# Sixty-four-row products of a hybrid backbone, cut into 64x64 quarters of the TensorE array

## Chip, core and metric

The kernel runs on one core of a Trainium2 chip. The metric is the device time of one execution in microseconds, the median of three runs. Another time in this text is that of one profiled execution, and its span, which is the time from the first to the last recorded instruction.

## What is computed

A two-layer backbone works on 1024 latent and 256 context tokens (1280 in all) of width 1024, in fp32. Each layer normalizes and modulates the tokens, projects them, and gives the columns to four mixers (S5, mLSTM, differential attention, gated linear attention). One output projection and a squared-ReLU MLP follow. The parts that matter here, cut from the reference:

```python
# S5: 16 groups, 64 complex states and 16 channels each, two directions
bu_re = einsum('blgh,gph->blgp', u, bb_re)          # and bu_im
h = associative_scan(...)                            # h_t = lam * h_(t-1) + bu_t
y = einsum('blgp,ghp->blgh', h_re, c_re) - einsum('blgp,ghp->blgh', h_im, c_im)

# mLSTM: 4 heads of width 64, chunks of 128 tokens, two directions
c_chunk = einsum('bhcs,bhcsv,bhcsk->bhcvk', e, vc, kc)
# c_prev: the state before each chunk
sc  = einsum('bhctd,bhcsd->bhcts', qc, kc) * exp(dmat - m_t[..., None])
num = einsum('bhcts,bhcsv->bhctv', sc, vc) + a_int[..., None] * einsum('bhcvk,bhctk->bhctv', c_prev, qc)
den = sum(sc, -1) + a_int * einsum('bhck,bhctk->bhct', n_prev, qc)
h   = num / maximum(abs(den), exp(-m_t))[..., None]

def hybrid_layer(x_lat, x_ctx, ...):
    s5, ml, da, gl = s5_mixer(...), mlstm_mixer(...), diff_attention_mixer(...), gla_mixer(...)
    x = x + g1 * (concat([s5, ml, da, gl]) @ w_out)
    x = x + g2 * sq_relu_mlp(norm(x), mlp_w1, mlp_w2)
```

## The kernel before

The kernel is written as generators, one for each mixer, that record instructions in small steps; `beside` and `both` interleave the steps. A scheduler then places each engine's instructions by readiness and priority, so that the order on an engine isn't the order of the text: two products that stand side by side in a loop may end up apart.

The stages of a layer follow each other. The modulation and the norm come first, then the projections `z_steps` (tiles zp). In layer 0 the constants of S5 (`s5_prep`) are made beside them. S5 (`s5_mix`) and GLA (`gla_mix`) run beside the projections, too. Then attention (`da_mix`), mLSTM (`ml_mix`) and half of the output projection (wop, `p_out`) run side by side. The other half of the output projection follows, and the MLP (m1p and m2p, each weight as a sum of two parts, hence the three lines L1124 to L1126). During the MLP of layer 0 `split_side` steps the constants of S5 for layer 1 forward, one group in every eight weight tiles.

TensorE multiplies a stationary tile (up to 128 rows by 128 columns) with moving columns; rows are the partitions of both operands, the columns of the stationary tile become the partitions of the output. Most products use all 128 rows. Four kinds use 64, since two S5 groups, or two mLSTM heads, lie above each other in the 128 partitions:

- L267 in `s5_prep`, the S5 constants: `win` (64 rows, 128 columns) by 16 moving columns, into two banks s5pd, one for each half of the rows;
- L313 in `s5_mix.outputs`, the S5 outputs: `mout` (64 rows, 128 columns) by the states X, 160 moving columns in layer 0 and 128 in layer 1, added to the product of L308 in the two banks s5py;
- L804 in `ml_mix.scores`: keys by queries, 128 moving columns, banks mlst;
- L826 in `ml_mix.values`, the inter-chunk part: decayed queries (mlab) by the state C (mlC, 65 moving columns), added to the product of L821 in the two banks mlpn.

In each, the loop over the halves of the rows (`g2`, `R` or `hh`) is the innermost. The innermost lines of L313, for example:

```python
for g2 in range(2):
    R = slice(64 * g2, 64 * g2 + 64)
    pe.matmul(py[g2][:, 0:n], mout[R, d, r], X[R, d, r, c0:], start=False, stop=d == 1 and r == 1)
```

Others of the kernel's products use part of the array already: L788 (mlpu) and L518 (dapo) have 128 rows and 64 columns and alternate between the column halves, L1064 (glpo) has 64x64 quarters. Who reads the results of the four: ScalarE's copies L276 and L277 for s5pd, VectorE's L316 for s5py, L809 for mlst, L829 and L835 for mlpn.

Of the kernel before, what the change touches and what calls it, by code (L numbers as in the profile page):

```python
# [138 lines left out]
def s5_prep(env, P, l, s5s, s5v, nj=2):  # L139
# [4 lines left out]
    v, g, act, pe = nc.vector, nc.gpsimd, nc.scalar, nc.tensor  # L144
    dr = env.dram
    dt_ = lambda nm, sh: dr.tile(sh, F32, name=f"s5_{nm}{l}", tag=f"s5_{nm}{l}")
    o = Env()
# [63 lines left out]
    for j0 in range(0, 8, nj):  # L211
# [11 lines left out]
        while m < 160:  # L223
            n = min(m, 160 - m, 64)
# [10 lines left out]
        win = P.tile([128, 2, 2, nj, 8, 16], F32, tag="win", name="s5win", bufs=nj)  # L235
# [14 lines left out]
        for jj in range(nj):  # L250
            pt = env.bank("s5p", "s5pt")
# [8 lines left out]
        H2 = [slice(64 * g2, 64 * g2 + 64) for g2 in range(2)]  # L260
        pd = [env.bank("s5p", "s5pd") for _ in range(2)]
        for jj in range(nj):
            for d in range(2):
                c0 = 32 * d + 16 * jj
                for r, rhs in ((0, vv[:, 2, d, jj]), (1, cn[:, d, jj])):
                    for R, p in zip(H2, pd):
                        pe.matmul(p[:, c0:c0 + 16], win[R, d, r, jj].rearrange("p s h -> p (s h)"), rhs[R], start=r == 0, stop=r == 1)  # L267
        for jj in range(nj):
            c0 = 64 + 16 * jj
            for d in range(2):  # L270
# [7 lines left out]
        C = slice(32 * j0, 32 * j0 + 32 * nj)  # L278
# [6 lines left out]
def s5_mix(env, l, o, us5, dskip, gluw, glub, out_cb, need_ctx=True):  # L285
# [3 lines left out]
    v, g, act, pe = nc.vector, nc.gpsimd, nc.scalar, nc.tensor  # L289
    dr = env.dram  # L290
    c0 = 0 if need_ctx else 32
    n = 160 - c0
    gs5 = dr.tile([128, 16, 160], F32, name=f"gs5_{l}", tag=f"gs5_{l}")
    with tc.tile_pool(name=f"s5m{l}", bufs=1, side="right", reuse_waits="tile") as P:
# [8 lines left out]
        def outputs(j, mout, toep, X):  # L303

            Y = P.tile([128, 2, n], F32, tag="Y", name="s5Y", bufs=1)
            py = [env.bank("s5y", "s5py") for _ in range(2)]
            for g2 in range(2):
                pe.matmul(py[g2][:, 0:n], toep[:, g2], U[:, 2 * j + g2, c0:], start=True, stop=False)  # L308
            for d in range(2):
                for r in range(2):  # L310
                    for g2 in range(2):
                        R = slice(64 * g2, 64 * g2 + 64)
                        pe.matmul(py[g2][:, 0:n], mout[R, d, r], X[R, d, r, c0:], start=False, stop=d == 1 and r == 1)  # L313
            for g2 in range(2):
                gi = 2 * j + g2
                v.scalar_tensor_tensor(Y[:, g2, :], U[:, gi, c0:], dsk[:, gi:gi + 1], py[g2][:, 0:n], op0=ALU.mult, op1=ALU.add)  # L316
            y2 = P.tile([128, 2, n], F32, tag="y2", name="s5y2", bufs=1)
            act.activation(y2, Y, AF.Square)
            g.tensor_scalar(y2, y2, 0.044715, 1.0, op0=ALU.mult, op1=ALU.add)
            v.tensor_tensor(y2, y2, Y, op=ALU.mult)  # L320
            v.tensor_scalar(y2, y2, -25.0, None, op0=ALU.max)
            act.activation(y2, y2, AF.Exp, scale=-2.0 * math.sqrt(2.0 / math.pi))
            act.activation(y2, y2, AF.Ln, bias=1.0)
            act.activation(y2, y2, AF.Exp, scale=-1.0)
            v.tensor_tensor(y2, y2, Y, op=ALU.mult)
            nc.sync.dma_start(gs5[:, 2 * j:2 * j + 2, c0:], y2)
            yield 2

        todo = []
        for j in range(8):  # L330
# [6 lines left out]
            mout = P.tile([128, 2, 2, 128], F32, tag="mo", name="s5mo", bufs=2)  # L337
# [3 lines left out]
            X = P.tile([128, 2, 2, 160], F32, tag="X", name="s5X", bufs=2)  # L341
# [350 lines left out]
def ml_mix(env, l, gates, qk, V, O, convw, convb, gain, cmask, out_cb, need_ctx):  # L692
# [4 lines left out]
    v, g, act, pe = nc.vector, nc.gpsimd, nc.scalar, nc.tensor  # L697
# [3 lines left out]
    with tc.tile_pool(name=f"ml{l}", bufs=1, side="right", reuse_waits="tile") as P:  # L701
# [5 lines left out]
        qT = P.tile([128, 2, T], F32, name="mlqT")  # L707
        kT = P.tile([128, 2, T], F32, name="mlkT")
        big = lambda nm: P.tile([128, T + 3], F32, tag="big", name=nm, bufs=6)
        for i in (2, 0, 3, 1):  # L710
# [8 lines left out]
            n = T + 1 - t0  # L719
# [21 lines left out]
        with tc.tile_pool(name=f"mlw{l}", bufs=1, side="right", reuse_waits="tile") as P2:  # L741
# [56 lines left out]
            def scores(hp, c2):  # L798
                R_ = [slice(64 * hh, 64 * hh + 64) for hh in range(2)]
                pt = [env.bank("mls", "mlst") for _ in range(2)]  # L800
                for c in range(2):
                    t0 = 128 * (c2 + c)
                    for hh in range(2):
                        pe.matmul(pt[hh][:, 128 * c:128 * c + 128], kT[R_[hh], hp, t0:t0 + 128], qT[R_[hh], hp, t0:t0 + 128], start=True, stop=True)  # L804
                yield 1
                for hh in range(2):
                    for d in range(2):
                        e = S[hp]["E"][d, hh][:, c2:c2 + 2].rearrange("p a b -> p (a b)")
                        v.tensor_tensor(e, pt[hh][:, 0:256], e, op=ALU.mult)  # L809
                yield 1  # L810

            def values(hp, c2, tmp):
# [2 lines left out]
                pns = [env.bank("mlv", "mlpn") for _ in range(2)]  # L815
                cd = [(c, d) for c in range(c2, c2 + 2) for d in range(2)]
                o = lambda hh, c, d: pns[hh][:, 130 * (c - c2) + 65 * d:130 * (c - c2) + 65 * d + 65]

                for c, d in cd:
                    for hh in range(2):  # L820
                        pe.matmul(o(hh, c, d), s["E"][d, hh][:, c], vx[:, c, 2 * hp + hh], start=(c, d) == cd[0], stop=False)  # L821
                yield 1
                for c, d in cd:
                    for hh in range(2):
                        R_ = slice(64 * hh, 64 * hh + 64)
                        pe.matmul(o(hh, c, d), s["qa"][d][R_, 128 * c:128 * c + 128], s["C"][d][R_, c], start=False, stop=(c, d) == cd[-1])  # L826
                pns = [pn[:, 0:260].rearrange("p (c d e) -> p c d e", c=2, d=2) for pn in pns]
                for hh in range(2):
                    v.tensor_copy(dn[:, hh], pns[hh][:, :, :, 64])  # L829
# [883 lines left out]
```

## Time and profile before

| what | us |
|---|---|
| median of three runs (3724.34 to 3726.04) | 3724.48 |
| the profiled execution | 3719.97 |
| its span | 3718.2 |
| TensorE matmul (PE) busy | 3435.5 (92%) |
| TensorE weight load (PEld) busy | 2725.4 (73%) |
| VectorE (DVE) busy | 2228.8 (60%) |
| ScalarE (ACT) busy | 1309.4 (35%) |
| GpSimd (POOL) busy | 450.7 (12%) |

PE rows are matmuls and PEld rows the weight loads that belong to them; the two overlap, and matmuls overlap one another, so a busy PE isn't at its peak. A form like "64*128 64x16" reads: a stationary tile of 64 rows and 128 columns, and 64 rows of 16 moving columns. In a timeline neighbours of one kind are merged into a row with a count, and the time given is that from the start of the first to the end of the last.

### The profile page before, as it was taken

Reading aid. Unit: us, or ns where it says so; the run is one execution under the profiler, and the core shown is the slowest. Engines: PE = TensorE matmul, PEld = TensorE weight load, DVE = VectorE, ACT = ScalarE, POOL = GpSimd, SP = SyncE. Lnnn points to the kernel's source line nnn. Section 1 sums busy time; section 2 is a strip of 40 time slices with the busy share of each in tenths; the row PEclk is TensorE's granted clock in tenths of the full one; section 3 lists DMA queues with packets and bytes.
Section 4 is the critical chain, followed back from the end, with each engine's and each line's share of the span. In section 5 each row is a group of like instructions: output and inputs, shape, how many; then the busy total and the mean of one; then the engine's idle time right before and its main releaser. Section 6 shows DMA issues by size and latency. Waiting matters only on the chain. (4 is left out here: it accounts for less than half of the span.)

```text
span 3718.2 us, 53487 instructions
## 1 busy us (share of the span) xinstructions
PE 3435.5 (92%) x20338; PEld 2725.4 (73%) x20338; DVE 2228.8 (60%) x5455; ACT 1309.4 (35%) x2457; POOL 450.7 (12%) x520
## 2 busy tenths in 40 slices
PE   6989998798889999999999798988889899999998
PEld 3867767576658888888888476867677578888885
DVE  9654685877659855455544637486788543333334
ACT  4223434766542121212121522435676431222222
POOL 2121221222100000000000123120222000000000
PEclk8979999898899999999999998999889899999999
DMA  5665324655461221222111265314653611111112
GB/s 216 230 205 154 129 77 133 214 183 166 141 208 57 90 82 69 81 74 86 61 39 42 102 201 161 120 57 143 213 167 104 205 46 51 46 51 46 52 47 78
DMA packets 233959, 430.23 MB, mean 116 GB/s; under 512 B 47415, under 2 KB 135911, under 8 KB 233447
## 3 DMA queue, kind: packets, MB, share of 16 engines
q1 hardware_dynamic: 192806, 381.03, 31.2%
q10 hardware_dynamic: 35520, 30.52, 2.6%
q0 software_dynamic: 5376, 15.28, 1.2%
q8 instruction: 160, 2.62, 0.3%
q14 instruction: 97, 0.79, 0.1%
HBM read 316.88 MB, written 109.86 MB: 115 GB/s over the span
## 5 line engine op out<-in xcount | busy, mean ns | idle before, releaser
L1562 DVE SCALAR_TENSOR_TENSOR X<-m2p,mods,X 128x256 f32<-128x256 f32 (+1 forms) x512 | 345.7, 683 | 345.1 <-PE m2p L1126 344.6
L1115 ACT CAST whi<-raw 128x1024 fp32r<-128x1024 f32 x182 | 191.1, 1050 | 919.8 <-PE m2p L1125 638.0
L1124 PE MATMUL m2p<-hidhi,whi 128*128 128x512 f32 (+1 forms) x1280 | 473.8, 372 | 3.5 <-DVE X L1562 2.8
L1124 PE MATMUL m1p<-h2hi,whi 128*128 128x512 f32 (+1 forms) x1280 | 474.3, 371 | 0.2 <-ACT h2hi L1209 0.2
L1125 PE MATMUL m1p<-h2lo,whi 128*128 128x512 f32 (+1 forms) x1280 | 473.6, 370 | 0.0
L1125 PE MATMUL m2p<-hidlo,whi 128*128 128x512 f32 (+1 forms) x1280 | 473.1, 370 | 0.0
L1126 PE MATMUL m2p<-hidhi,wlo 128*128 128x512 f32 (+1 forms) x1280 | 472.2, 370 | 0.8 <-DVE wlo L1116 0.8
L1126 PE MATMUL m1p<-h2hi,wlo 128*128 128x512 f32 (+1 forms) x1280 | 472.6, 370 | 0.0
L1116 DVE TENSOR_TENSOR wlo<-raw,whi 128x1024 fp32r<-128x1024 f32 x182 | 224.7, 1235 | 313.2 <-ACT whi L1115 301.2
L1124 PEld LDWEIGHTS m2p<-hidhi,whi 128*128 128x128 f32 x1280 | 241.6, 189 | 59.6 <-issue 8.6
L1124 PEld LDWEIGHTS m1p<-h2hi,whi 128*128 128x128 f32 x1280 | 243.1, 190 | 46.2 <-ACT whi L1115 4.2
L1126 PEld LDWEIGHTS m2p<-hidhi,wlo 128*128 128x128 f32 x1280 | 241.2, 188 | 46.4 <-issue 3.4
L1125 PEld LDWEIGHTS m1p<-h2lo,whi 128*128 128x128 f32 x1280 | 243.4, 190 | 40.8 <-DVE h2lo L1210 0.8
L1126 PEld LDWEIGHTS m1p<-h2hi,wlo 128*128 128x128 f32 x1280 | 243.2, 190 | 40.3 <-issue 0.4
L1125 PEld LDWEIGHTS m2p<-hidlo,whi 128*128 128x128 f32 x1280 | 241.6, 189 | 42.0 <-issue 2.2
L1124 PE MATMUL zp<-hhi,whi 128*128 128x512 f32 (+1 forms) x664 | 254.2, 383 | 11.6 <-ACT zst L1237 9.6
L487 DVE TENSOR_SCALAR_CACHE_REDUCE das<-daps 128x512 f32<-128x512 f32 (+1 forms) x400 | 226.0, 589 | 58.4 <-PE daps L486 55.0
L1125 PE MATMUL zp<-hlo,whi 128*128 128x512 f32 (+1 forms) x664 | 251.2, 378 | 5.6 <-DVE hlo L1205 5.2
L1126 PE MATMUL zp<-hhi,wlo 128*128 128x512 f32 (+1 forms) x664 | 249.5, 376 | 0.0
L1576 DVE TENSOR_TENSOR rl<-rl,m1p 128x256 f32<-128x256 f32 (+1 forms) x160 | 100.8, 631 | 177.1 <-ACT rl L1575 177.1
L498 ACT ACTIVATE das<-das,danm 128x1280 f32<-128x1280 f32 x128 | 174.3, 1362 | 42.7 <-DVE danm L496 42.3
L486 PE MATMUL daps<-daqk,daqk 128*128 128x512 f32 (+1 forms) x400 | 153.3, 447 | 38.0 <-DVE das L487 36.6
(460 smaller groups left out, 6671.3 us busy)
## 6 DMA issues: line engine op xcount, KB each, us to landing
raw<-w SPq DMA_DIRECT2D x136, 512.0 KB
adaw<-ada_w SPq DMA_DIRECT2D x96, 512.0 KB
whl<-wsp SPq DMA_DIRECT2D x80, 512.0 KB
wsp<-whl SPq DMA_DIRECT2D x32, 512.0 KB
raw<-wz SPq DMA_DIRECT2D x30, 512.0 KB
daqk<-da_st SPq DMA_DIRECT2D x24, 640.0 KB
mlE<-ml_rows SPq DMA_DIRECT2D x16, 640.0 KB
xn<-xo SPq DMA_DIRECT2D x72, 128.0 KB
```

The source lines that it names most:

```text
L486: pe.matmul(p[:, 0:b - a], Q[m][:, 128 * qt:128 * qt + 128], K[m][:, a:b], start=True, stop=True)
L487: v.tensor_scalar(s[:, a:b], p[:, 0:b - a], -1.0, None, op0=ALU.mult, op1=ALU.min, accum_out=pm[:, i:i + 1])
L498: act.activation(s[:, :k1], s[:, :k1], AF.Exp, bias=nm[:, 0:1], scale=-1.0, accum_out=sm[m])
L1115: nc.scalar.copy(hi, raw)
L1116: nc.vector.tensor_tensor(lo, raw, hi.bitcast(F32), op=ALU.subtract)
L1124: pe.matmul(out, ah, bh, start=i == 0, stop=False)
L1125: pe.matmul(out, ah, bl, start=False, stop=False)
L1126: pe.matmul(out, al, bh, start=False, stop=i == n - 1)
L1562: nc.vector.scalar_tensor_tensor(X[b][:, m], p[:, :n], mod(l, 5, s)[:, m:m + 1], X[b][:, m], op0=ALU.mult, op1=ALU.add)
L1576: nc.vector.tensor_tensor(rl[:, :n], rl[:, :n], p[:, :n], op=ALU.mult)
```

## The change

Each of the four products is cut into two that have 64 of the 128 stationary columns each and write 64 partitions of the same bank. The loop over the column halves (`M`) stands outside the loop over the row halves, so that in the text four quarters follow each other: rows 0 to 63 and 64 to 127 with the first 64 columns, then both with the last 64. Operands, banks, sums and moving columns stay the same. The number of matmuls of these lines doubles: in both layers together 128, 128, 72 and 144 become 256, 256, 144 and 288.

```diff
@@ s5_prep
-                    for R, p in zip(H2, pd):
-                        pe.matmul(p[:, c0:c0 + 16], win[R, d, r, jj].rearrange("p s h -> p (s h)"), rhs[R], start=r == 0, stop=r == 1)
+                    for M in H2:
+                        for R, p in zip(H2, pd):
+                            pe.matmul(p[M, c0:c0 + 16], win[R, d, r, jj].rearrange("p s h -> p (s h)")[:, M], rhs[R], start=r == 0, stop=r == 1)
@@ s5_mix, outputs
+            H2 = [slice(64 * i, 64 * i + 64) for i in range(2)]
...
-                    for g2 in range(2):
-                        R = slice(64 * g2, 64 * g2 + 64)
-                        pe.matmul(py[g2][:, 0:n], mout[R, d, r], X[R, d, r, c0:], start=False, stop=d == 1 and r == 1)
+                    for M in H2:
+                        for g2 in range(2):
+                            pe.matmul(py[g2][M, 0:n], mout[H2[g2], d, r, M], X[H2[g2], d, r, c0:], start=False, stop=d == 1 and r == 1)
@@ ml_mix, scores
-                    for hh in range(2):
-                        pe.matmul(pt[hh][:, 128 * c:128 * c + 128], kT[R_[hh], hp, t0:t0 + 128], qT[R_[hh], hp, t0:t0 + 128], start=True, stop=True)
+                    for M in R_:
+                        for hh in range(2):
+                            pe.matmul(pt[hh][M, 128 * c:128 * c + 128], kT[R_[hh], hp, t0 + M.start:t0 + M.stop], qT[R_[hh], hp, t0:t0 + 128], start=True, stop=True)
@@ ml_mix, values
+                H2 = [slice(64 * i, 64 * i + 64) for i in range(2)]
...
-                    for hh in range(2):
-                        R_ = slice(64 * hh, 64 * hh + 64)
-                        pe.matmul(o(hh, c, d), s["qa"][d][R_, 128 * c:128 * c + 128], s["C"][d][R_, c], start=False, stop=(c, d) == cd[-1])
+                    for M in H2:
+                        for hh in range(2):
+                            pe.matmul(o(hh, c, d)[M], s["qa"][d][H2[hh], 128 * c + M.start:128 * c + M.stop], s["C"][d][H2[hh], c], start=False, stop=(c, d) == cd[-1])
```

Since the scheduler places the instructions, two places show what stands in TensorE's row now. The first is in the MLP of layer 0, at one group of the S5 constants (adap is the modulation of layer 1, s5pt a transpose; the lines below the change have moved by up to four). Before:

```order
L253 MATMUL s5pt<-ident,s5win 128x128 x4
L267 MATMUL s5pd<-s5vv,s5win 128x16
L267 MATMUL s5pd<-s5cn,s5win 128x16
L267 MATMUL s5pd<-s5vv,s5win 128x16
L267 MATMUL s5pd<-s5cn,s5win 128x16
L274 MATMUL s5pd<-s5vv,s5win 16x16
L274 MATMUL s5pd<-s5cn,s5win 16x16
L274 MATMUL s5pd<-s5vv,s5win 16x16
L274 MATMUL s5pd<-s5cn,s5win 16x16
L1124 MATMUL m1p<-h2hi_10593,whi 128x256
```

And now, at the same place:

```order
L253 MATMUL s5pt<-ident,s5win 128x128 x4
L268 MATMUL s5pd<-s5vv,s5win 64x16 x2
L268 MATMUL s5pd<-s5cn,s5win 64x16 x2
L268 MATMUL s5pd<-s5vv,s5win 64x16 x2
L268 MATMUL s5pd<-s5cn,s5win 64x16 x2
L275 MATMUL s5pd<-s5vv,s5win 16x16
L275 MATMUL s5pd<-s5cn,s5win 16x16
L275 MATMUL s5pd<-s5vv,s5win 16x16
L275 MATMUL s5pd<-s5cn,s5win 16x16
L1128 MATMUL m1p<-h2hi_10841,whi 128x256
```

All of these four products, before and now, belong to one bank and so to one half of the rows; the other bank's four follow some matmuls of the MLP later. What follows each other now is the two column halves of a product.

The second place is TensorE in the attention stretch of layer 1, at one pair of chunks of mLSTM (the number of mlpn tells the bank and with it the half of the rows). Before:

```order
L518 MATMUL dapo_24612<-dawT_25688,davt_23641 64x128
L826 MATMUL mlpn_25703<-mlC_24273,mlab_24725 128x65
L826 MATMUL mlpn_25704<-mlC_24273,mlab_24725 128x65
L826 MATMUL mlpn_25703<-mlC_24274,mlab_24729 128x65
L826 MATMUL mlpn_25704<-mlC_24274,mlab_24729 128x65
L826 MATMUL mlpn_25703<-mlC_24273,mlab_24725 128x65
L826 MATMUL mlpn_25704<-mlC_24273,mlab_24725 128x65
L826 MATMUL mlpn_25703<-mlC_24274,mlab_24729 128x65
L826 MATMUL mlpn_25704<-mlC_24274,mlab_24729 128x65
L486 MATMUL daps_25746<-daqk1_25603,daqk0_25605 128x256
```

And now the first ten of the sixteen that stand there:

```order
L520 MATMUL dapo_24988<-dawT_26096,davt_24017 64x128
L830 MATMUL mlpn_26111<-mlC_24649,mlab_25101 64x65
L830 MATMUL mlpn_26112<-mlC_24649,mlab_25101 64x65
L830 MATMUL mlpn_26111<-mlC_24649,mlab_25101 64x65
L830 MATMUL mlpn_26112<-mlC_24649,mlab_25101 64x65
L830 MATMUL mlpn_26111<-mlC_24650,mlab_25105 64x65
L830 MATMUL mlpn_26112<-mlC_24650,mlab_25105 64x65
L830 MATMUL mlpn_26111<-mlC_24650,mlab_25105 64x65
L830 MATMUL mlpn_26112<-mlC_24650,mlab_25105 64x65
L830 MATMUL mlpn_26111<-mlC_24649,mlab_25101 64x65
L830 MATMUL mlpn_26112<-mlC_24649,mlab_25101 64x65
```

Here the banks alternate before and now; each pair of banks stands there twice in a row now, once for each half of the columns.

## Rows read from the trace of the kernel before

**Rows 1.** The page, part 1: busy time of each engine.

```profile
PE 3435.5 (92%) x20338; PEld 2725.4 (73%) x20338; DVE 2228.8 (60%) x5455; ACT 1309.4 (35%) x2457; POOL 450.7 (12%) x520
```

**Rows 2.** Stretches: start and end, length, busy time per engine (instructions), clock, DMA.

```profile
55.00:70.00 15.00, 10.88 (x75) 10.13 (x75) 14.97 (x50) 5.54 (x11) 6.83 (x7) 0.50 0.18 73
70.00:165.00 95.00, 90.89 (x590) 72.93 (x591) 70.23 (x247) 32.68 (x71) 13.29 (x28) 0.94 0.57 193
215.00:330.00 115.00, 100.28 (x546) 77.79 (x547) 81.11 (x195) 32.52 (x75) 41.01 (x59) 0.78 0.56 177
700.00:850.00 150.00, 134.37 (x1101) 106.03 (x1097) 118.48 (x392) 98.64 (x218) 35.63 (x34) 0.97 0.61 197
1150.00:1970.00 820.00, 816.92 (x4443) 681.68 (x4442) 482.65 (x1273) 150.45 (x262) 35.08 (x68) 0.99 0.21 73
2650.00:2760.00 110.00, 105.33 (x874) 84.98 (x873) 89.69 (x295) 72.48 (x144) 25.13 (x25) 0.98 0.62 202
2760.00:2900.00 140.00, 124.29 (x911) 96.58 (x910) 110.87 (x359) 86.97 (x184) 33.10 (x28) 0.85 0.41 132
```

**Rows 3.** The chain, 2660 to 2890 us, by line; line L826 alone, 2650 to 2900.

```profile
by line: PE dapo L518 13.3%; PE daps L486 12.2%; PE dapt L527 11.4%; issue 6.7%; PE mlpn L821 5.9%; PE mlpn L826 5.7%; DVE das L487 5.2%; PE wop L1124 5.1%; PE wop L1125 4.5%; PE wop L1126 4.3%; DVE das L506 4.1%; DMA xo<-xl 2.3%; PE mlst L
2650.00:2900.00 250.00, 14.77 (x128) 12.46 (x128) 0.91 0.50 163
```

**Rows 4.** Weight loads by line and form: count, busy us, mean ns, idle before.

```profile
L826 PEld LDWEIGHTS mlpn<-mlC,mlab 64*128 64x128 f32 x288 | 26.3, 201 | 8.7 <-issue 4.2 <-POOL mlab L795 2.6
L788 PEld LDWEIGHTS mlpu<-mlvx,mlkw 128*64 128x64 f32 x288 | 17.1, 146 | 24.2 <-issue 15.5 <-DVE mlkw L769 2.6 <-DVE mlC L789 1.3
L1064 PEld LDWEIGHTS glpo<-glA,glv 64*64 64x64 f32 x288 | 5.8, 133 | 3.1 <-issue 3.1
```

**Rows 5.** Timeline of weight loads: S5 constants of layer 1, then of layer 0.

```profile
1240.57 0.29 PEld L267 LDWEIGHTS s5pd<-s5vv,s5win 64*128 64x128 f32 x2 [0.17 <-issue]
1240.79 0.30 PEld L267 LDWEIGHTS s5pd<-s5cn,s5win 64*128 64x128 f32 x2
...
1241.56 0.11 PEld L274 LDWEIGHTS s5pd<-s5vv,s5win 64*16 64x16 f32 x2
...
60.74 0.54 PEld L267 LDWEIGHTS s5pd<-s5cn,s5win 64*128 64x128 f32 x2
61.17 0.54 PEld L267 LDWEIGHTS s5pd<-s5vv,s5win 64*128 64x128 f32 x2
```

**Rows 6.** Timeline of weight loads: mLSTM, inter-chunk part (L826) and scores (L804).

```profile
2866.71 0.96 PEld L826 LDWEIGHTS mlpn<-mlC,mlab 64*128 64x128 f32 x8
...
2749.21 0.97 PEld L826 LDWEIGHTS mlpn<-mlC,mlab 64*128 64x128 f32 x16 [0.17 <-issue]
2750.25 0.30 PEld L486 LDWEIGHTS daps<-daqk,daqk 128*128 128x128 f32 x2
...
946.48 0.52 PEld L804 LDWEIGHTS mlst<-mlqT,mlkT 64*128 64x128 f32 x4 [0.17 <-issue]
...
891.97 0.52 PEld L804 LDWEIGHTS mlst<-mlqT,mlkT 64*128 64x128 f32 x8 [0.36 <-issue]
```

**Rows 7.** Timeline of weight loads: lines that use 64 columns already.

```profile
494.93 0.32 PEld L1064 LDWEIGHTS glpo<-glA,glv 64*64 64x64 f32 x16 [0.17 <-issue]
...
708.72 0.31 PEld L788 LDWEIGHTS mlpu<-mlvx,mlkw 128*64 128x64 f32 x6 [0.17 <-DVE whl L1457]
...
2736.62 0.85 PEld L518 LDWEIGHTS dapo<-dawT,davt 128*64 128x64 f32 x16 [0.17 <-issue]
```

**Rows 8.** Weight loads of the S5 outputs: timeline, then the line's row.

```profile
294.29 1.11 PEld L313 LDWEIGHTS s5py<-s5X,s5mo 64*128 64x128 f32 x8 [0.17 <-issue]
...
317.13 1.12 PEld L313 LDWEIGHTS s5py<-s5X,s5mo 64*128 64x128 f32 x16 [0.17 <-issue]
...
L313 PEld LDWEIGHTS s5py<-s5X,s5mo 64*128 64x128 f32 x256 | 34.5, 236 | 31.4 <-DVE s5X L374 20.0 <-DVE s5X L379 4.9 <-issue 3.7
```

**Rows 9.** Waits over the whole span: engine and line, releaser, us, times, longest.

```profile
PEld daps L486 <- DVE das L487: 57.0, 67, 7.8
```

## Prediction

> **What bounds the kernel now.** I read the page first, then the stretches, then single stretches of TensorE's weight loads. The page says that TensorE is the engine to look at: 92% busy, with the next engine, VectorE, at 60% [rows 1]. An average over stages doesn't price an edit, so the table by stretches comes next [rows 2]. The changed products stand in five kinds of stretch, and each has its own limit:
>
> - the MLP of layer 0, where the S5 constants of layer 1 are slipped in (1150 to 1970 us): TensorE is busy for 816.92 of 820 us [rows 2]. It is the bound, and what it no longer does comes off the end in full;
> - the projections with the S5 constants of layer 0 (70 to 165 us): TensorE 90.89 of 95 [rows 2];
> - attention, mLSTM and the first half of the output projection side by side (700 to 990 and 2650 to 2900 us): TensorE 96% busy at best and 89% at worst in the three rows, VectorE 79 to 82% [rows 2]. The chain over 2660 to 2890 us runs mostly through TensorE, the changed line L826 alone with 5.7% [rows 3]; that is 13.1 of the 14.77 us that this line is busy there [rows 3];
> - the S5 outputs (215 to 330 us, and again in layer 1): TensorE is busy for 100.28 of 115 us, and where it idles it waits for VectorE's X (L374, 20.0 us) [rows 2, 8].
>
> So the question is how long TensorE is occupied by the four changed lines, and how much of that the two mixed kinds of stretch pass on.
>
> **How such products run today.** An fp32 product is two records of weight load and matmul in the trace: line L826 has 288 records for 144 products [rows 4]. The queue of weight loads shows the rest. In the S5 constants the eight records of one group (four products) have weight loads that start in pairs 0.22 us apart, 1240.57, 1240.79 and so on until L274's at 1241.56, so one every 0.11 us: they use the same 64 rows, one after the other, since the scheduler put all products of one bank first [rows 5]. In mLSTM's inter-chunk part eight records of one row half take 0.96 us, and sixteen records that alternate between the two row halves take 0.97 us [rows 6]. The scores show the same with four and eight records in 0.52 us [rows 6]. Alternating row halves already run side by side; one slot of 0.11 us ((0.97 - 0.20) / 7, with the mean load's 0.20 us [rows 4]) holds two records then, and one otherwise. With 16 and 65 moving columns the slot is the weight load's, since it is the same for both; with 160 columns it is the matmul's: eight records in 1.11 us and sixteen in 1.12 us, 0.133 us a slot [rows 8].
>
> **What a slot costs when the weights have 64 columns.** The trace has it next door. GLA's 64x64 products (L1064) issue sixteen records in 0.32 us: with 0.133 us for the last load [rows 4], four slots take 0.187 us, less some 0.02 us by which the four of a slot are staggered, so 0.055 us a slot, and each slot holds four records [rows 7]. The 64-column loads of L788, 65 moving columns, give (0.31 - 0.146) / 3 = 0.055 us for two records that share all rows and differ in the column half (two of the eight are missing from the trace) [rows 4, 7]. With 128 moving columns the matmul sets the pace: sixteen records of L518 in 0.85 us, (0.85 - 0.14) / 7 = 0.101 us for two [rows 7]. I take 0.056 us for short products, 0.101 us for 128 columns, 0.133 us for 160.
>
> **The change part by part.** I counted slots in the order of the instructions, before and after: in every unbroken piece the records of the busiest tile.
>
> S5 constants (L267). 64 products in layer 1 become 128, but the two column halves of a product stand next to each other, so the number of slots stays 128 and each shrinks from 0.11 to 0.056: 6.9 us, all in the saturated MLP, all passed on. One group should go from the 0.99 us between its first load and L274's to some 0.55 us. Layer 0 has 96 slots. 32 of them lie at 60 to 68 us, where the granted clock is 0.50, the 1.2 GHz level, and take 0.21 us each [rows 2, 5]; VectorE is busy for 14.97 of the 15 us from 55 to 70 [rows 2] and lets nothing through, so I put them at 0 (bound: 32 x 0.105 = 3.4 us). The other 64 slots give 3.5 us, of which TensorE's 96% pass on 3.2.
>
> mLSTM inter-chunk part (L826). 196 slots of 0.11 become 188 of 0.056: 21.6 - 10.5 = 11.1 us. That fits the trace, where the loads of this line are busy for 26.3 us [rows 4]: 196 x 0.11 and, in 37 pieces, 0.09 us more for the last load, and a few slots at the lower clock.
>
> mLSTM scores (L804). 116 slots before and after; with 128 moving columns each goes from 0.11 to 0.101, 1.0 us, and each of 34 pieces starts some 0.05 us earlier since its first load is half as long: 1.7 us. Together 2.7 us.
>
> S5 outputs (L313). The matmul sets the pace here, so slots stay as long as they are. Only the first load of 31 pieces gets shorter, 1.6 us, and a little in layer 1, say 2.0 us; VectorE's X ends last, so I pass on 0.8 (bounds 0 and 2.6).
>
> What the attention stretches pass on of 11.1 + 2.7 = 13.8 us: by the busy share 0.89 to 0.96, by the chain 13.1 of 14.77 us for L826, and against it the scores' bank: TensorE's loads waited 57.0 us for VectorE's L487 in both layers [rows 9], and whatever makes TensorE earlier there only makes that wait longer. I take 0.75, 10.3 us, with bounds 0 and 13.8.
>
> Nothing is moved on purpose, but the scheduler places every instruction anew. With the changed lines left out, 732 of 16,763 places in TensorE's order hold another instruction than before, mostly a neighbour's, most of them in the two attention stretches; SP and POOL move less. No DMA is added and no wait that wasn't there. The consumers (L276, L316, L809, L829) wait for the last of more records; the last record of a piece ends earlier by the sums above. I put the moves at 0, with 4 us to either side, half of the longest single wait of the scores for VectorE (7.8 us) [rows 9].
>
> Sum: 6.9 + 3.2 + 10.3 + 0.8 = 21.2 us. The profiled execution took 3719.97 us (span 3718.2), so 3698.8; the median of the three runs is 3724.48, 4.5 us above it, and against that median, which the result will be compared with, it is **3703**.
>
> Two rules of the Trainium skill speak against such a split. First the rows: L1064's sixteen loads start within 0.19 us, 12 ns apart on average, with 64 moving columns [rows 7]. "TensorEngine Tiling (Array Packing)", Performance Considerations, Instruction Overhead, says that every matmul carries some 60 cycles and that one shouldn't take the tiling factor from a dimension that is already small. By that, at the upper clock, an estimate of 25 ns for each record, a slot of four would take 0.10 us and not 0.056, and mLSTM's inter-chunk part would gain 3 us instead of 11.1; with 0.75 of it passed on the kernel would take 3709, inside the forecast's own range below. The rows show less than that, so the sum keeps 0.056.
>
> **The rivals.**
>
> *The attention loop swallows its share.* Scores, VectorE's minimum (L487) and ScalarE's exponential form a ring with two banks; if the ring sets the pace in those stretches, the 13.8 us become longer waits of L486 for L487 and only the S5 constants are left: 3724.5 - 6.9 - 3.2 = 3714. For it: 57.0 us of waits for L487 [rows 9]. Against it: 96% TensorE in 2650 to 2760 us [rows 2], and the chain.
>
> *The new order costs what it saves.* Two further waits of 7.8 us in the attention stretches, at the places where mLSTM's pieces now stand in another row, take away 15.6 us: 3719. For it: most of the moved places lie there. Against it: the moves are between neighbours.
>
> *The column halves of one row half take turns* (slower, and then the change doesn't do what it says). Rows 0 to 63 would then serve one quarter after the other, and each slot holds two records, as today, with twice as many records. Short products gain nothing (two loads of 0.056 for one of 0.11); the long ones pay for the second pass over the moving columns: L804 116 x 0.101 less the 1.0 and 1.7 us, some +9 us, L313 108 slots x 0.133 in layer 0 and 76 x 0.101 in layer 1, +22 us. With 0.75 and 0.5 of that passed on, 18 us: 3742. It decides as soon as the second column half starts more than half a slot after the first. Against it: L788's pairs share all 128 rows and their loads take 0.055 us for two; L1064's four quarters go together.
>
> The Trainium skill has a rule of this kind: "TensorE: Matmul & The Clock Gate", Part 3, What overlaps and what doesn't, says that a weight load overlaps running matmuls only where the row group differs. By that rule this rival would come true. The rows of L788 and L518 show it otherwise for column halves.
>
> **How the numbers follow.** A difference of 0.2%, 7.4 us, is about the least that a measurement of this kernel can tell from no change; faster is below 3717.0. Forecast 0.66 (its own range 3696 to 3710), ring 0.15, new order 0.13, taking turns 0.06. The first two are faster by the bound, and so is a little of the third: 0.82 faster, 0.12 the same, 0.06 slower. The range reaches down to everything passed on (6.9 + 3.5 + 13.8 + 2.6 + 4 = 31 us: 3693) and up past the ring to the edge of the new order: 3693 to 3717.
>
> **What would show it.** In the changed profile: in the MLP's stretch eight products of the S5 constants load in about 0.53 us per group, sixteen records; L826's pieces of 32 records take about 0.6 us against 1.04; L313's pieces keep 1.1 us; the records of the four lines double, and TensorE is busy for some 20 us less in all. In the attention stretches, waits of L486 for L487 that grow by more than 4 us mean the ring. If the loads of a piece start 0.056 us apart one by one and not in twos or fours, the halves take turns, and the step "a slot holds both column halves" is wrong.

## The result and the profile after

The changed kernel takes 3684.25 us (median of four executions, 3676.74 to 3686.84; the kernel before, beside it, 3724.41). The ratio is 0.9894 with a 95% interval of 0.9871 to 0.9917, so it is some 40 us faster, about twice the 21 us that the prediction summed up, and outside its range of 3693 to 3717. In the profiled execution the span goes from 3718.2 to 3684.5 us and the mean granted clock from 0.952 to 0.955.

The page of the changed kernel, part 1, as in [rows 1]:

```profile
PE 3393.9 (92%) x21282; PEld 2677.8 (73%) x21282; DVE 2228.0 (60%) x5455; ACT 1309.5 (36%) x2457; POOL 448.6 (12%) x520
```

TensorE has 944 records more and is busy for 41.6 us less; the other engines stand where they were. "Some 20 us less" was expected. The records themselves are not the reason, for they came out as the prediction had them. The timeline of weight loads of the changed kernel (start, length, line, tiles, shape, count), S5 constants of layer 1, then a piece of mLSTM's inter-chunk part, then one of the S5 outputs, to be held against [rows 5, 6, 8]; a few lines were added above them, so L267 is L268 now, L274 L275, L826 L830, L313 L315, L804 L807:

```profile
1230.47 0.19 PEld L268 LDWEIGHTS s5pd<-s5vv,s5win 64*64 64x64 f32 x4 [0.17 <-issue]
1230.59 0.20 PEld L268 LDWEIGHTS s5pd<-s5cn,s5win 64*64 64x64 f32 x4
...
1231.05 0.11 PEld L275 LDWEIGHTS s5pd<-s5vv,s5win 64*16 64x16 f32 x2
...
2722.13 0.56 PEld L830 LDWEIGHTS mlpn<-mlC,mlab 64*64 64x64 f32 x32 [0.17 <-issue]
2722.76 0.42 PEld L488 LDWEIGHTS daps<-daqk,daqk 128*128 128x128 f32 x3
...
301.57 1.02 PEld L315 LDWEIGHTS s5py<-s5X,s5mo 64*64 64x64 f32 x32 [0.17 <-issue]
```

A group of the S5 constants takes 0.58 us up to L275 (1230.47 to 1231.05; 0.99 before, 0.53 to 0.55 expected), an inter-chunk piece 0.63 us to the next load (1.04 before, 0.6 expected), and an S5 output piece takes 1.02 us (1.12 before; its first and its last load are shorter). All pieces of a line together, each from its first product to the next product of another line: S5 constants in the MLP, here with the 16-column products of L274 behind them, 20.88 us before and 14.14 after (6.7 us; 6.9 forecast); inter-chunk part 30.65 and 17.37 (13.3 us; 11.1 forecast); scores 20.1 and 19.2 (0.9 us; 2.7 forecast).

So where do the other 20 us come from? The next rows cut three stretches at their first and last product: the S5 outputs of layer 0 (L308's first to L313's last product), the MLP of layer 0 in the piece of [rows 2], and mLSTM in layer 1 (L804's first to L826's last). The columns are those of [rows 2]; the last but two is the granted clock. The kernel before, outputs and mLSTM:

```profile
216.20:318.20 102.00, 87.28 (x436) 65.28 (x434) 76.92 (x188) 27.78 (x65) 37.99 (x54) 0.75 0.59 189
2666.90:2883.70 216.80, 201.22 (x1544) 160.47 (x1545) 175.94 (x565) 139.87 (x290) 53.87 (x49) 0.91 0.46 146
```

The changed kernel, outputs, MLP and mLSTM:

```profile
212.60:306.00 93.40, 78.39 (x563) 56.65 (x562) 77.32 (x188) 27.59 (x64) 37.21 (x54) 0.82 0.65 206
1150.00:1970.00 820.00, 817.32 (x4628) 681.91 (x4628) 478.53 (x1220) 156.14 (x272) 35.16 (x68) 1.00 0.22 73
2643.50:2847.70 204.20, 185.85 (x1737) 146.51 (x1737) 173.72 (x565) 138.82 (x290) 56.12 (x49) 0.96 0.50 156
```

The granted clock rose in all three: 0.75 to 0.82, 0.99 [rows 2] to 1.00, 0.91 to 0.96. The trace knows two levels, 0.50 and 1.00 (1.2 and 2.4 GHz), so a mean of 0.75 over 102 us is 51 us at the lower one. That is what the prediction had no term for. The experiments ask whether it belongs to the change.

### The profile page after: what moved, and what is told of

Same layout as the page of the kernel before. It is cut to its first block, busy times and chain, and to the rows that moved or that the text cites. A ratio compares the mean times of both kernels' runs of the same rounds, so it can differ in the third digit from the quotient of the medians.

```text
span 3684.5 us, 55377 instructions
## 1 busy us (share of the span) xinstructions
PE 3393.9 (92%) x21282; PEld 2677.8 (73%) x21282; DVE 2228.0 (60%) x5455; ACT 1309.5 (36%) x2457; POOL 448.6 (12%) x520
## 5 line engine op out<-in xcount | busy, mean ns | idle before, releaser
L1128 PE MATMUL zp<-hhi,whi 128*128 128x512 f32 (+1 forms) x664 | 254.5, 384 | 11.3 <-ACT zst L1241 9.6
```

What stands on the lines that cost most here:

```text
L1128: pe.matmul(out, ah, bh, start=i == 0, stop=False)
```

## The theories

- **Theory 1:** the slots gave what was forecast; the rest is the clock. Half-array products leave TensorE's clock at the lower level for some of the time, and with quarters there is less of that.
- **Theory 2:** the rest is work that the scheduler moved, or a larger share passed on in the attention stretches.
- **Theory 3:** half-clock time falls where it likes, in any kernel, and the traces of before and after differ in it by chance.

## One part at a time

e1 has the S5 constants alone in quarters, e2 the S5 outputs, e3 the scores, e4 the inter-chunk products; the rest of each is the kernel before. The hunk of e1 stands below; the others are the corresponding hunks of the diff. What the expectations call the feed-forward stretch is the MLP of layer 0:

```diff
-                    for R, p in zip(H2, pd):
-                        pe.matmul(p[:, c0:c0 + 16], win[R, d, r, jj].rearrange("p s h -> p (s h)"), rhs[R], start=r == 0, stop=r == 1)
+                    for M in H2:
+                        for R, p in zip(H2, pd):
+                            pe.matmul(p[M, c0:c0 + 16], win[R, d, r, jj].rearrange("p s h -> p (s h)")[:, M], rhs[R], start=r == 0, stop=r == 1)
```

> The S5 constants alone in quarters, everything else as before. Slots alone: 7 groups in layer 0's feed-forward stretch at about 0.85 us less each, 6 us, and some 3 us at 58 to 62 us, so about 9 us less than before (3715 where before is 3724). Theory 1 (what the whole change gave beyond its slots is the granted clock, and a shorter stretch of narrow products leaves fewer half-clock windows): the four windows at 0.50 in the feed-forward stretch go as well, 6.6 us more, about 16 us less in all, and the S5 output stretch of layer 0 keeps its 51 us at 0.50. Theory 2 (the work that the schedule moved made the rest): the windows at 0.50 stay as many as before, and 6 to 9 us in all. Theory 3 (the clock's dips fall by chance, whatever the kernel): the half-clock time changes with either sign in stretches that this edit doesn't touch, by 10 us of windows or more.

> The S5 outputs alone in quarters. Slots alone: 2 us less over both layers. Theory 1: the S5 output stretch of layer 0 (before: 51 us at 0.50) loses some 17 us of half clock, worth 8 us, so about 10 us less in all; the feed-forward stretch keeps its four windows. Theory 2: 0 to 2 us less. Theory 3: half-clock time of the stretch anywhere between 34 and 51 us, and other stretches differ as much.

> The mLSTM scores alone in quarters. Slots alone: the forecast's 2.7 us by 0.75, 2 us less. Theory 1: 0 to 5 us more than that, as windows at 0.50 in the second layer's attention go. Theory 2: what the attention stretches pass on is their moved work, 0 to 2 us. Theory 3: as for the first run.

> The mLSTM inter-chunk products alone in quarters. Slots alone: 576 pieces in 18 groups, 11.1 us by 0.75, 8 us less. Theory 1: second-layer attention also loses some 20 us of its 37 us at 0.50, 10 us more, so 8 to 18 us less. Theory 2: 8 to 11 us with the clock as before. Theory 3: as for the first run.

Measured against the kernel before on the same chip (3725.31 us):

| kernel | median us | ratio | interval | ratio in us |
|---|---|---|---|---|
| e1, S5 constants | 3702.93 | 0.9947 | 0.9927 to 0.9966 | -19.7 |
| e2, S5 outputs | 3714.16 | 0.9975 | 0.9962 to 0.9988 | -9.3 |
| e3, scores | 3714.27 | 0.9979 | 0.9964 to 0.9993 | -7.8 |
| e4, inter-chunk | 3705.05 | 0.9952 | 0.9936 to 0.9969 | -17.9 |

Each part alone gives more than its slots: the forecast had 10, 0.8, 2 and 8 us. Where it does so is in the table below, one line for each trace, those of the later experiments too, with the length of a stretch in us and the part of it at the lower clock, summed from the trace's records of the granted clock (half-clock time from here on). The traces come from more than one chip (e1 to e8 from one, e9 to e11 and e12 to e15 from two others).

| trace | S5 outputs, layer 0 | MLP, layer 0 | mLSTM, layer 1 |
|---|---|---|---|
| before, first | 101.9 / 51 | 991.4 / 20 | 216.9 / 37 |
| before, e8 | 102.1 / 48 | 993.6 / 27 | 217.2 / 37 |
| before, e12 | 94.4 / 31 | 994.6 / 27 | 216.9 / 37 |
| before, e14 | 101.2 / 48 | 994.3 / 27 | 213.9 / 31 |
| e1, constants alone | 100.2 / 48 | 979.8 / 10 | 217.0 / 37 |
| e2, outputs alone | 92.3 / 31 | 994.1 / 27 | 216.5 / 37 |
| e3, scores alone | 102.2 / 51 | 990.8 / 24 | 211.0 / 20 |
| e4, inter-chunk alone | 101.2 / 48 | 987.9 / 17 | 203.5 / 14 |
| e10, filler | 97.5 / 41 | 993.0 / 24 | 212.8 / 24 |
| e11, before with constants twice | 101.2 / 48 | 1017.0 / 55 | 210.9 / 20 |
| after, first | 93.4 / 34 | 980.0 / 10 | 204.1 / 17 |
| after, e5 | 92.1 / 34 | 979.8 / 10 | 206.5 / 20 |
| after, e13 | 92.9 / 31 | 980.1 / 10 | 207.3 / 20 |
| after, e15 | 93.0 / 37 | 979.9 / 10 | 201.9 / 14 |
| e6, after with constants twice | 91.5 / 31 | 988.6 / 14 | 209.5 / 24 |
| e7, after without the scores | 97.7 / 51 | 979.0 / 7 | 204.6 / 17 |
| e9, after, rows first | 92.5 / 34 | 979.9 / 10 | 204.9 / 17 |

Theory 1 fits best. With the constants alone the MLP is 12 to 15 us shorter than in the traces of before and has 10 us at the lower clock, as with the whole change, while the other two stretches stay as before; with the outputs alone only the first column moves; e3 and e4 move the last. Theory 2 would have the clock as before and falls with these columns.

Chance has a part, too, so the columns have to be read as a whole. In the MLP eight traces have half-array products of the constants, once each, and 17 to 27 us at the lower clock (17 in e4, which has no edit there); seven have quarters once, and 7 to 10 us. In the S5 output stretch seven of eight traces with half-array products have 48 to 51 us (31 in e12; e10 isn't counted, since it adds products there), and seven of eight with quarters 31 to 37 (51 in e7). In layer 1's mLSTM six of eight traces with both of its products as before have 31 to 37 us (24 in e10, 20 in e11), and the nine others 14 to 24. So the MLP tells the two forms apart in every trace, the other two stretches in most.

The third stretch may also say why the four parts add up to 54.7 us and the whole to 40: in e3 and e4 alike the half-clock time there goes from 37 to 20 or less, and that can be had only once. For e3 this is argued and not shown: its 211.0 us with 20 at the lower clock are those of e11 (210.9 and 20), which leaves the stretch as it was.

## The change again, and without the scores

> The changed kernel once more, beside the kernel before on one chip. If the extra gain is of the change (theories 1 and 2), some 40 us less again, with the half-clock time of the feed-forward stretch of layer 0 near 10 us, of the S5 output stretch of layer 0 near 34 us and of the second layer's mLSTM stretch near 17 us, as in the first trace of it. If the half-clock windows fall by chance (theory 3), these stretches come out elsewhere, by 10 us and more, and the gain moves towards the forecast's 21 us.

> The kernel before, profiled once more. Theory 1: half-clock time as in its first trace within a window or two: 20 us in the feed-forward stretch of layer 0, 51 us in the S5 output stretch of layer 0, 37 us in the second layer's mLSTM stretch. Theory 3: these numbers move by 10 us or more, as between the two kernels.

e5 measures 3683.20 us, 0.9891 (0.9868 to 0.9914); the size of the gain stands, and with it theory 3 as the whole cause falls: the three stretches repeat (table). e8, the kernel before once more, took 3727.71 us in its one execution.

> The changed kernel with the mLSTM scores as before. The scores alone gave 8 us and the inter-chunk products alone 18 us, but both took the half-clock time of the second layer's mLSTM stretch from 37 us to 20 and 14, the whole change to 17. Theory 1: that gain can be had only once, so without the scores this kernel loses only their slots, 2 to 3 us (3687 where the change has 3685). If the parts' gains add up as slots do (theory 2): 8 us slower than the change, 3692.

e7 undoes one hunk (L807 with `for hh` alone and all 128 columns, as before). It measures 3682.12 us, 0.9889 (0.9864 to 0.9915): not slower than the change beside it (e5, 3683.20) at all. The 8 us that the scores gave alone are not added on top, which theory 1 says and the sum of slots doesn't. But its S5 output stretch has 51 us at the lower clock with the quarters in. That stretch, then, isn't settled by the form of its products alone.

## What takes the clock down in the MLP

There the change is cleanest, since nothing but the S5 constants differs. e6 issues each quarter product of the constants twice in the changed kernel, e11 each half-array product twice in the kernel before. One edit makes both:

```diff
-                for r, rhs in ((0, vv[:, 2, d, jj]), (1, cn[:, d, jj])):
+                for r, rhs in ((0, vv[:, 2, d, jj]), (1, cn[:, d, jj])) * 2:
```

> The changed kernel with each quarter product of the S5 constants issued twice (the second pass starts its sums anew, so the outputs are the same). A group's narrow stretch is then about as long as before the change (some 1.0 us before, 0.57 us after, about 1.15 us here). By slots alone 7 groups in the feed-forward stretch cost 0.57 us each, 4 us, and the cold group some 1.8 us: 984 us for that stretch, 6 us in all. Theory 1 with the length of the narrow stretch as the cause: the four windows at 0.50 come back as well, 5 us more: the stretch takes 988 to 991 us with some 20 us at half clock, and about 11 us in all. If it is the form of the products and not their length: half-clock time stays near 10 us and the stretch at 984 us.

> The kernel before with its half-array products of the S5 constants issued twice, the same doubling that was tried on the changed kernel. Per piece 8 records more at 0.107 us, 0.86 us; 128 records in the feed-forward stretch, 13.7 us, which takes 1005 to 1007 us if the half-clock time there stays at 20 to 27 us. If half-clock time follows the number of these half-array products: 10 to 20 us more at half clock and 1010 to 1017 us. The cold group adds 3.4 us, so 3741 to 3755 in all.

e6: 3700.90 us, 0.9934 (0.9912 to 0.9956). Its pieces of constants take 21.6 us of the MLP, as long as before the change (20.9), yet 14 us of the stretch lie at the lower clock and not the 20 to 27 of before. That speaks against the form that I gave theory 1 in the expectation, the length of the narrow stretch; it is one trace, and e4 has 17 with half-array products. The 4 us expected by slots were also too small: a quarter piece got 0.47 us longer and its 256 additional records cost 7.5 us. In all e6 takes 17.7 us more than e5, where 6 or 11 were expected; the MLP has 9 us of that, and mLSTM in layer 1, which it doesn't change, 3.

e11: 3751.02 us, 1.0082 (1.006 to 1.0104). 55 us of the MLP lie at the lower clock where the kernel before has 20 to 27, and the stretch takes 1017 us: half-clock time does follow the number of half-array products, by 28 us or more where 10 to 20 were expected. What it is about such a product that does this stays open. Its 128 additional records cost 18 us of pieces (39.1 for 20.9) and not 13.7, since some of them run at the lower clock themselves. The same 12 us, from a group of constants on, in four kernels (windows, columns as above). The kernel before:

```profile
1364.00:1376.00 12.00, 12.00 (x82) 10.68 (x79) 7.33 (x26) 2.03 (x8) 3.08 (x5) 0.86 0.51 162
```

The changed kernel:

```profile
1351.00:1363.00 12.00, 12.00 (x106) 10.38 (x105) 9.54 (x41) 2.46 (x8) 3.83 (x6) 1.00 0.56 177
```

e6:

```profile
1349.00:1361.00 12.00, 12.00 (x133) 10.56 (x132) 8.93 (x39) 2.16 (x8) 3.86 (x6) 1.00 0.50 165
```

e11:

```profile
1384.00:1396.00 12.00, 12.00 (x84) 11.20 (x81) 4.69 (x17) 1.66 (x7) 3.08 (x5) 0.72 0.51 162
```

TensorE is busy for all of the 12 us in each, with the form and the number of its products and the clock differing: 0.86, 1.00, 1.00, 0.72. The timeline of weight loads of e11 shows the fall within the second group of that window:

```profile
1387.87 0.30 PEld L267 LDWEIGHTS s5pd<-s5vv,s5win 64*128 64x128 f32 x2
1388.10 0.47 PEld L267 LDWEIGHTS s5pd<-s5cn,s5win 64*128 64x128 f32 x2
1388.44 0.54 PEld L267 LDWEIGHTS s5pd<-s5vv,s5win 64*128 64x128 f32 x2
```

Two loads go from 0.30 to 0.54 us, and the loads of 128 columns after them stay longer until the clock comes back. The kernel before shows the same after its second group, on products that aren't S5's (timeline of weight loads, the MLP's own):

```profile
1366.18 0.19 PEld L1125 LDWEIGHTS m1p<-h2lo,whi 128*128 128x128 f32 x1
1366.30 0.19 PEld L1126 LDWEIGHTS m1p<-h2hi,wlo 128*128 128x128 f32 x1
...
1368.17 0.34 PEld L1126 LDWEIGHTS m1p<-h2hi,wlo 128*128 128x128 f32 x1
...
1370.96 0.33 PEld L1124 LDWEIGHTS m1p<-h2hi,whi 128*128 128x128 f32 x1
1371.17 0.33 PEld L1125 LDWEIGHTS m1p<-h2lo,whi 128*128 128x128 f32 x1
```

The MLP's own loads start 0.12 us apart before the fall and 0.21 behind it (2.78 us for 13 steps from 1368.39 to 1371.17), so each us at the lower level costs this stretch some 0.44 us, an estimate from these rows.

So the price of a half-array product is not only its slot; some of the full products behind it pay as well. The Trainium skill ("TensorE: Matmul & The Clock Gate", Part 1, HAM oscillation) tells of the clock falling where matmuls wait for transfers. This trace differs: the clock falls here with TensorE busy for 12.00 of 12 us.

## More work in the S5 output stretch

e10 is the kernel before with each Toeplitz product of the S5 outputs (L308, 128 rows) issued twice, to fill TensorE's waits in that stretch:

```diff
-            for g2 in range(2):
-                pe.matmul(py[g2][:, 0:n], toep[:, g2], U[:, 2 * j + g2, c0:], start=True, stop=False)
+            for k, g2 in ((0, 0), (0, 1), (1, 0), (1, 1)):
+                pe.matmul(py[g2][:, 0:n], toep[:, g2], U[:, 2 * j + g2, c0:], start=True, stop=k == 0)
```

> The kernel before with more work for TensorE in the S5 output stretch: each of its products with the Toeplitz block is issued twice, the second starting the sum anew (same outputs). Per group 4 records more at 0.136 us (0.27 at half clock), 8 groups: 4.4 to 8.7 us in layer 0's stretch, less some 2 to 4 us that fall into waits for the state; 3.5 us at most in layer 1. If the clock follows how steadily TensorE works (theory 1): the stretch of layer 0 has at most 41 us at half clock where before has 48 to 51, and it takes 97 to 103 us where before takes 102. If not: 48 us or more, and 104 to 111 us.

It measures 3718.44 us, 0.9995 (0.9983 to 1.0006): 64 more records, some 6 us of TensorE (pieces of L308: 26.6 us before, 32.4 here), for nothing that can be measured. The trace has what theory 1 wanted, 41 us at the lower clock and 97.5 us in all, but that is inconclusive: the mean clock of its 12 executions, 0.9519, is hardly above that of the kernel before beside it (0.9513), and e12, the kernel before as it is, had 94.4 us and 31. What it does show stands in the last column. In layer 1's mLSTM stretch e10 issues the same 1544 matmuls as the first trace of before, in the same order, and its rows read (e10):

```profile
2666.00:2878.80 212.80, 196.47 (x1544) 156.80 (x1545) 175.80 (x565) 139.88 (x290) 53.80 (x49) 0.94 0.48 149
```

4.0 us less than before's row, at 0.94 for 0.91. e11 has the same matmuls in the same order there, too, and takes 210.9 us with 20 at the lower clock. So this stretch can lose half-clock time without an edit there.

## Two more traces of each

e12 and e14 are the kernel before, e13 and e15 the changed one, all without an edit.

> The kernel before, a third trace. If the stretches' half-clock time belongs to the kernel: 48 to 51 us in the S5 output stretch and 20 to 27 us in the feed-forward stretch of layer 0, 37 us in the second layer's mLSTM stretch. If the last falls by chance, as e10 and e11 suggest: 20 to 38 us there, and 211 to 217 us long.

> The changed kernel, a third trace. If the stretches' half-clock time belongs to the kernel: 31 to 34 us in the S5 output stretch, 10 us in the feed-forward stretch, 17 to 20 us in the second layer's mLSTM stretch. If it falls by chance: up to 51 us in the first (as e7 had), up to 37 us in the last.

> The kernel before, a fourth trace. If half-clock time belongs to the kernel: 48 to 51 us, 20 to 27 us and 37 us in the three stretches; if by chance, the last anywhere from 20 to 38 us.

> The changed kernel, a fourth trace. If half-clock time belongs to the kernel: 31 to 34 us, 10 us and 17 to 20 us in the three stretches; if by chance, the first up to 51 us and the last up to 37 us.

The MLP is settled: 20 to 27 us at the lower clock in four traces of before, 10 in four of after, with no overlap. In layer 1's mLSTM stretch it is 31 to 37 against 14 to 20; among kernels that leave that stretch as it was, e10 and e11 reach down to 24 and 20, so part of the difference there may be chance. The S5 output stretch has 31 us once among four of before and 31 to 37 in all four of after. The means of four traces (3722.0 and 3684.4 us of span):

| stretch | before us | after us | difference | us at the lower clock before, after |
|---|---|---|---|---|
| S5 constants of layer 0 and projections, up to the S5 outputs | 157.7 | 152.8 | -4.9 | 32, 27 |
| S5 outputs, layer 0 | 99.9 | 92.9 | -7.1 | 44, 34 |
| mLSTM, layer 0 | 255.3 | 249.5 | -5.8 | 35, 34 |
| MLP, layer 0 | 993.5 | 979.9 | -13.5 | 26, 10 |
| S5 outputs, layer 1 | 110.7 | 108.7 | -2.0 | 22, 28 |
| mLSTM, layer 1 | 216.2 | 205.0 | -11.3 | 36, 18 |
| all the rest | 1888.7 | 1895.6 | +6.9 | 168, 175 |

## Does the order of the quarters matter?

e9 turns the four loops round, so that the two quarters on the same rows are neighbours; for the inter-chunk part, and the other three likewise:

```diff
-                    for M in H2:
-                        for hh in range(2):
+                    for hh in range(2):
+                        for M in H2:
                             pe.matmul(o(hh, c, d)[M], s["qa"][d][H2[hh], 128 * c + M.start:128 * c + M.stop], s["C"][d][H2[hh], c], start=False, stop=(c, d) == cd[-1])
```

> The changed kernel with the four loops turned round, so that quarters of the same 64 rows stand next to each other (rows 0, rows 0, rows 1, rows 1) where the change alternates them. If only the sum of quarters counts, since rows of before at 7 ns apart hold for either neighbour: within 3 us of the changed kernel (3680 to 3687) and pieces of 32 inter-chunk weight loads still near 0.63 us. If neighbours must lie on different rows (the rival rule of the prediction, in its mild form: only every second pair overlaps): these pieces go to 0.8 to 1.0 us, half to all of the slots' gain of 23 us is lost, and the time is 3695 to 3707.

It measures 3684.71 us, 0.9902 (0.9885 to 0.9919), the same as the change. A piece of 32 in its timeline of weight loads:

```profile
2717.67 0.56 PEld L830 LDWEIGHTS mlpn<-mlC,mlab 64*64 64x64 f32 x32 [0.17 <-issue]
2718.30 0.42 PEld L488 LDWEIGHTS daps<-daqk,daqk 128*128 128x128 f32 x3
```

0.56 us and 0.63 to the next load, to the hundredth as in the changed kernel. (All pieces of the line together take 20.6 us for the change's 17.4, since the scheduler cut them into 43 where the change has 36; the whole time doesn't show it.) Loads of one piece start 6 or 7 ns apart within a four and 35 to 40 ns from four to four. The S5 constants of the changed kernel say the same: the scheduler put the two column halves of one product next to each other there, on the same rows, and their loads start 6 or 7 ns apart. The rule of the Trainium skill that the prediction weighed ("TensorE: Matmul & The Clock Gate", Part 3, What overlaps and what doesn't: a load overlaps running matmuls only across row groups) doesn't describe this: by it two neighbours on the same rows would take turns. That the quarters *alternate*, as the change has them, is not what gains.

## Why the prediction was wrong, point by point

- **"A slot holds both column halves, 0.056 us."** Right. Pieces came out at 0.58 and 0.63 us; the rival of the halves that take turns is dead, in e9 too. The rival estimate of 0.10 us for a slot of four (3709) is out with it.
- **S5 constants, layer 1, 6.9 us.** The slots are right (6.7), and passed on in full. The stretch is 13.5 us shorter. The other 6.8 us go with 15.4 us fewer at the lower clock, 0.44 us for each, which is what the MLP's loads lose at that level (0.12 us apart for 0.21). This is the step that failed: **every duration was taken at the clock of its row, and the sum had no term for the clock: it was put at nothing without a reason.** The rows held the hint: a clock of 0.99 in the MLP with TensorE busy for 99.6% of it, 0.78 and 0.85 elsewhere [rows 2].
- **S5 constants, layer 0, 3.2 us with nothing for the 32 slots at 60 to 68 us.** The nothing was right. These slots got 3.0 us shorter (the start of the first group to the first product of the projections takes 8.0 us in each trace of before and 5.0 in each of after), but the second product of the projections waits for VectorE's hlo, and that wait got 3.0 us longer. Waits of TensorE from 55 to 75 us (in total, times, longest), the kernel before and the changed one:

```profile
PE zp L1125 <- DVE hlo L1205: 3.5, 2, 3.2
PE zp L1129 <- DVE hlo L1209: 6.5, 2, 6.2
```

From the first group to that product it is 11.8 us in each of the eight traces. What the stretch passes on, 4.9 us in the mean, lies behind it: the other 64 slots, whose pieces took 7.7 us in the first trace of before and 4.3 in that of after (3.4 us; 96% of the forecast's 3.5 are 3.3 and not 3.2), and some 1.5 us more beside 4.9 us fewer at the lower clock.

- **Attention stretches, 13.8 us of slots by 0.75.** Layer 0 tests this, since its half-clock time stays (35 and 34 us): 8.1 us of slots (pieces of L826 and L804: 17.0 and 12.3 us before, 9.8 and 11.4 after), 5.8 us passed on, 0.7. In layer 1 6.1 us of slots go with 11.3 us; at 0.7 it is 4.3 us of slots and 7 us of clock for 17.9 us at the lower level. That fits the traces with 20 us at the lower clock each: e11, where the stretch has no edit, takes 210.9 us, e5 and e13 take 206.5 and 207.3. How much of those 7 us is the change's and how much chance is open. Within the term the sizes were off both ways: the inter-chunk part gave 13.3 us for 11.1, the scores 0.9 for 2.7, since with 128 moving columns their slot doesn't shrink: 0.109 us between its loads before and after. (The forecast's 0.101 averages in the first step of L518's loads, 0.055 us; its other steps are 0.109, too.)
- **The ring.** Not the limit, though it took its part. The row of waits, changed kernel:

```profile
PEld daps L488 <- DVE das L489: 61.6, 77, 10.4
```

57.0 us before [rows 9], 56.9 to 58.3 in four traces, and 61.4 to 62.2 after. The 4 us that I had put down as the sign of the ring were reached, and the stretches got shorter all the same: a wait that grows by 4 us beside 14 us of slots is the share not passed on, no bound.

- **S5 outputs, 0.8 us.** Measured 7.1 and 2.0 us. At the same half-clock time slots give 1.5 us (e12 and e13, 31 us each) to 4.2 us (before and e7, 51 us each) in layer 0; the rest goes with the clock, mostly but, by e7 and e12, not always with the form of the products. Layer 1 got shorter with 6 us more at the lower clock.
- **Moves, 0 with 4 to either side.** The rest of the kernel got 6.9 us longer, 3.6 of it in layer 1's GLA, and has 7 us more at the lower clock. That is beyond the 4 us to either side, and its cause wasn't followed.

By terms: 6.7 (constants, MLP), 3.4 (constants, layer 0), 5.8 and 4.3 (attention), 1.5 and 2.0 (outputs) less 6.9 are some 17 us of slots and moves, for 21.2 forecast. The clock has 6.8, 1.5, 5.6 and 7, together some 21 us, for 0 forecast. This split is an estimate. Counted over the whole span, the four traces of after have 37 us fewer at the lower clock (326 for 363), which at the MLP's 0.44 is 16 us. Another reading comes near: over 50 timed executions of the kernel before, between 3709 and 3738 us, a mean clock higher by 0.001 goes with 2.6 us less; e5's five executions stand 0.0056 above those of before beside them (0.9558 and 0.9502), 15 us of 40. That is a correlation without a direction, so it bounds nothing.

No kernel here beats the change beyond its interval: e7 (0.9889) and e9 (0.9902) lie with it.

## What to carry over

Before you price a product that fills half of the array, look at the granted clock of its stretch and of the stretch behind it: a value below 1.00 where TensorE never waits is time that such an edit may give back, on top of its slots. Give it a term with bounds: nothing on one side, and on the other all of the time at 0.50 times what a us of it costs there (0.44 us in the MLP here). Take several traces before you believe where the clock falls. Which neighbours overlap is read from the starts of the loads.

## What was not expected of the hardware

- The clock falls with TensorE busy for 12.00 of 12 us. Half-array products went before it (e11: 55 us at the lower level in the MLP, before: 20 to 27, quarters: 10), and quarter products of the same total length less of it (e6: 14, one trace).
- Four quarters, with rows alternating or not, start 6 to 7 ns apart, and with 65 moving columns the next four 35 to 40 ns later.
- A stretch with the same matmuls in the same order can differ by 4 to 6 us (layer 1's mLSTM in e10 and e11 and in the first trace of before), with 14 to 17 us fewer at the lower clock.
